# A hybrid layer's first 512 tokens: half of the weight's columns first, squares on ACT, sums later, the norm one group later

## The chip, the cores and the metric

One core of a Trainium2 chip runs the whole layer in one launch. Its engines are named as in the profile: PE (TensorE, matrix products; PEld is its weight load), DVE (VectorE), ACT (ScalarE), POOL (GpSimd) and SP (SyncE, which here only issues transfers). The metric is the device time of one execution in microseconds (us), the median of several runs.

## The reference

The layer normalises its input, multiplies it by one combined weight, sends parts of the result through two token mixers (a gated DeltaNet and a dilated window attention), and adds the projected result to the input. Only the first lines bear on the change:

```python
def rms_norm(x, w):
    xf = x.astype(jnp.float32)
    return xf * lax.rsqrt(jnp.mean(xf * xf, axis=-1, keepdims=True) + EPS) * w.astype(jnp.float32)
...
    h = rms_norm(x, norm_w).astype(x.dtype)
    proj = h @ w_in
```

x is 2048 tokens by 1024 channels, the weight 1024 by 4104, all in float32. The stage that changes computes columns 1536 to 2055 of the projection: the 512 columns of z, the gate of the DeltaNet branch, and eight columns for its decay and beta.

## The kernel before

Every product is made of three: an operand is split into a high part in a shorter float format (fp32r) and a low part, the rest; high by high, high by low and low by high are summed in PSUM. The norm's factor per token (rstd) is applied behind the products, when a PSUM bank is read, so the products need not wait for it.

The first stage runs over four blocks of 512 tokens (tb 0 to 3); x comes in transposed, in pieces of 128 channels by 512 tokens. Piece n is block n // 8, channels of step kt = n % 8. The 520 columns of the weight are taken in two halves of 260 (b 0 and 1), each in eight row blocks of 128 channels.

The helpers of the stage, lines 243 to 320:

- `z_load(kt)` loads a row block of the weight, all 520 columns, into one of four raw buffers (lines 239 and 240: row block kt + 4 comes into the buffer of row block kt). `z_high(kt, b)` casts a half of it to its high part on ACT (`wh`), `z_low(kt, b)` makes the low part on DVE (`wl`).
- `x_in(n)` loads a piece of x into one of six buffers (`xr`), so it waits until piece n - 6 has been read by all. `x_high(n)` on ACT and `x_low(n)` on DVE make its parts (`xh`, `xl`). `x_square(n)` squares it, on POOL for block 0 and on ACT for the others, into `acc` (step 0 of a block) or into one of two buffers `sq`; `x_add(n)` adds that to `acc` on DVE.
- `parts(n)` is square, high part, sum, low part of piece n, and the load of piece n + 6.
- `x_norm(tb)` sums `acc` over the channels with eight small products on PE (`pm`), then DVE (`ssq`) and POOL (`rstd`, a power) make the factor. `x_row` transposes it on PE and copies it (`rr`), `x_row_out` writes it out and reads it back for later stages. All of these use the one PSUM bank `pm`.
- `z_out` reads a finished bank through Silu on ACT with the factor as its scale into one of five buffers (`zt`), copies the eight extra columns on DVE for b = 1 (`ba`), and stores `zt` by a transfer that SP issues (`zs_d`).

The opening, lines 326 to 349, makes the products of tokens 0 to 511 with the half b = 0: eight steps of twelve products (four token tiles, three products each) in four banks, kept open over all steps. Within a step the second half's parts are made too, for row blocks 0 to 3, since their buffers are wanted for row blocks 4 to 7:

```python
    for kt in range(KT):
        x_high(kt)
        z_low(kt, 0)
        x_low(kt)
        if kt + 1 < KT:
            z_high(kt + 1, 0)
        x_square(kt)
        x_add(kt)
        if kt < 4:
            z_high(kt, 1)
            z_low(kt, 1)
            z_load(kt + 4)
```

Then come 28 groups of 24 products (lines 354 to 384), each one bank: groups 0 to 3 are tokens 0 to 511 with b = 1, groups 4 to 11 are block 1 with b = 0 and 1, and so on. With the groups 0 to 3 go two pieces of x each (pieces 8 to 15), with the others one. Groups 1 and 2 use two banks of another pool (`pj`), all others five banks in turn (`pz`), so group 3 needs the bank that token tile 0 had in the opening. In block 0 the norm stands behind the products of group 0 and the first `z_out` behind those of group 1; the banks wait in a list until then.

From line 222 to line 388 every engine's queue, SP's among them, keeps the order in which the lines are written (`pin`); behind line 388 a scheduler sets the order. All transfers spoken of here but one are issued by SP, in order, and an issue that waits for its buffer holds those behind it. Fourteen warm-up products (line 230) run ahead of the first ones.

Of the kernel before, what the change touches and what calls it, by code (L numbers as in the profile page):

```python
# [8 lines left out]
F32 = mybir.dt.float32  # L9
F32R = mybir.dt.float32r  # L10
AF = mybir.ActivationFunctionType
ALU = mybir.AluOpType
# [4 lines left out]
P = 128  # L17
S = 2048
D = 1024
KT = 8  # L20
# [61 lines left out]
def dap(t, off, dims):  # L82
    return bass.AP(tensor=t.tensor, offset=t.offset + off, ap=[list(d) for d in dims])


def hybrid(tc, xT, x, norm_w, w_in, conv_w, a_log, dt_bias, dn_norm_w, q_norm_w, k_norm_w,
# [37 lines left out]
    dma = nc.sync.dma_start  # L124
    adma = nc.scalar.dma_start

    dr, _ = pool("dr", space=DRAM)
# [18 lines left out]
    cst, _ = pool("cst")  # L146
# [34 lines left out]
    wp, wp_g = pool("wp", side="right")  # L181
# [15 lines left out]
    def proj_tok(ps, ws, tt, n, c0=0):  # L197
        tb, o = divmod(tt, 4)
        jobs = [(kt, x_, w_) for kt in range(KT) for x_, w_ in ((xh, 0), (xh, 1), (xl, 0))]
        for j, (kt, x_, w_) in enumerate(jobs):  # L200
            w = ws[kt][w_][:, ws[kt][2], :n]
            nc.tensor.matmul(ps[:, c0:c0 + n], x_[tb][:, kt, o * P:(o + 1) * P], w, start=j == 0, stop=j == len(jobs) - 1)
# [14 lines left out]
    sp0, sp0_g = pool("sp0")  # L217
# [5 lines left out]
    nc = engines  # L223
    dma = nc.sync.dma_start
# [5 lines left out]
    for _ in range(14):  # L230
# [4 lines left out]
    zw = {(b, g): tuple((wp if b + g < 2 else sp0).tile([P, 4, 260], F32R, name=n if b + g < 2 else n + "z",  # L235
                                                        bufs=3 if b + g < 2 else 1) for n in ("wh", "wl"))
          for b, g in ((0, 0), (0, 1), (1, 0), (1, 1))}
    wz = [[(*zw[b, kt // 4], kt % 4) for kt in range(KT)] for b in range(2)]
    raws = [wp.tile([P, 4, 260], F32, name="wraw", bufs=2).rearrange("p (k b) n -> p k (b n)", k=2) for _ in range(2)]
    raws = [raws[k // 2 % 2][:, k % 2] for k in range(KT)]  # L240
    xraw, acc = {}, {}

    def z_load(kt):
        dma(raws[kt], w_in[kt * P:(kt + 1) * P, 1536:2056])

    def z_high(kt, b):
        nc.scalar.activation(zw[b, kt // 4][0][:, kt % 4], raws[kt][:, b * 260:(b + 1) * 260], AF.Copy)

    def z_low(kt, b):
        wh, wl = zw[b, kt // 4]  # L250
        nc.vector.tensor_tensor(wl[:, kt % 4], raws[kt][:, b * 260:(b + 1) * 260],
                                wh[:, kt % 4].bitcast(F32), op=ALU.subtract)

    def x_in(n):
        tb, kt = divmod(n, KT)
        if n < 4 * KT:
            xraw[n] = xr = sp0.tile([P, 512], F32, name="xr", bufs=XRB)
            last_x[0] = dma(xr, xT[kt * P:(kt + 1) * P, tb * 512:(tb + 1) * 512])

    def x_high(n):  # L260
        tb, kt = divmod(n, KT)
        nc.scalar.mul(xh[tb][:, kt], xraw[n], nw[:, kt:kt + 1])

    def x_square(n):
        tb, kt = divmod(n, KT)
        if kt == 0:
            acc[tb] = sq = sp0.tile([P, 512], F32, name="acc", bufs=2)
        else:
            acc[tb, kt] = sq = sp0.tile([P, 512], F32, name="sq", bufs=2)
        if tb == 0:  # L270
            nc.gpsimd.tensor_tensor(sq, xraw[n], xraw[n], op=ALU.mult)
        else:
            nc.scalar.activation(sq, xraw[n], AF.Square)

    def x_low(n):
        tb, kt = divmod(n, KT)
        nc.vector.scalar_tensor_tensor(xl[tb][:, kt], xraw[n], nw[:, kt:kt + 1], xh[tb][:, kt].bitcast(F32),
                                       op0=ALU.mult, op1=ALU.subtract)

    def x_add(n):  # L280
        tb, kt = divmod(n, KT)
        if kt:
            nc.vector.tensor_tensor(acc[tb], acc[tb], acc.pop((tb, kt)), op=ALU.add)

    def parts(n):
        if n < 4 * KT:
            x_square(n)
            x_high(n)
# [12 lines left out]

    def x_row(tb):

        pr = psA.tile([P, 512], F32, name="pm", bufs=1)
        nc.tensor.transpose(pr[:4, :P], rstd[:, 4 * tb:4 * tb + 4], ident)
        rr = sp0.tile([4, P], F32, name="rr")
        nc.vector.tensor_copy(rr, pr[:4, :P])
        return rr

    def x_row_out(tb, rr):  # L310
        dma(dap(rstd_d, tb * 512, [[P, 4], [1, P]]), rr)
        dma(rstd_b[:, tb * 512:(tb + 1) * 512], dap(rstd_d, tb * 512, [[0, P], [1, 512]]))

    def z_out(tt, b, ps):
        zt = sp0.tile([P, 260], F32, name="zt", bufs=5)
        n = 260 if b == 0 else 252
        nc.scalar.activation(zt[:, :n], ps[:, :n], AF.Silu, scale=rstd[:, tt:tt + 1])
        if b:
            nc.vector.tensor_scalar(ba[:, :, tt], ps[:, 252:260], rstd[:, tt:tt + 1], None, op0=ALU.mult)
        dma(zs_d[tt * P:(tt + 1) * P, b * 260:b * 260 + n], zt[:, :n])  # L320

    XRB = 6
    last_x = [None]

    pz = [psZ.tile([P, 512], F32, name="pz", bufs=5) for _ in range(4)]
    for kt in range(4):
        z_load(kt)
        x_in(kt)
    x_in(4)
    z_high(0, 0)  # L330
    for kt in range(KT):
        x_high(kt)
        z_low(kt, 0)
        x_low(kt)
        if kt + 1 < KT:
            z_high(kt + 1, 0)
        x_square(kt)
        x_add(kt)
        if kt < 4:
            z_high(kt, 1)  # L340
            z_low(kt, 1)
            z_load(kt + 4)
        if kt == 0:
            x_in(5)
        x_in(kt + XRB)
        for i in range(4):
            for j, (x_, w_) in enumerate(((xh, 0), (xh, 1), (xl, 0))):
                nc.tensor.matmul(pz[i][:, :260], x_[0][:, kt, i * P:(i + 1) * P], wz[0][kt][w_][:, kt % 4, :260],
                                 start=kt == 0 and j == 0, stop=kt == KT - 1 and j == 2)
# [2 lines left out]
    waiting = [(i, 0, pz[i]) for i in range(4)]  # L352
    n = KT
    for g, (tb, b, i) in enumerate(groups):
        if g == 0:
            for kt in range(4, KT):
                z_high(kt, 1)
                z_low(kt, 1)
        if g in (1, 2):
            ps = psA.tile([P, 512], F32, name="pj", bufs=PJB)  # L360
        else:
            ps = psZ.tile([P, 512], F32, name="pz", bufs=5)
        proj_tok(ps, wz[b], 4 * tb + i, 260)
        for _ in range(2 if tb == 0 else 1):
            parts(n)
            n += 1
        k = g if tb == 0 else (g - 4) % 8
        if k == 0:
            x_norm(tb)
        if k >= 1:  # L370
            for w in waiting:
                z_out(*w)
            waiting = []
        waiting.append((4 * tb + i, b, ps))
        if k == 2:
            rr = x_row(tb)
        if k == 3:
            x_row_out(tb, rr)
        if g == 6:
            dma(cw, conv_w)  # L380
            for w, src in enumerate((q_norm_w, k_norm_w)):
                for s_ in range(2):
                    dma(qw[s_ * CH:(s_ + 1) * CH, w:w + 1], dap(src, 0, [[1, CH], [1, 1]]))
            dma(dnw, dap(dn_norm_w, 0, [[1, P], [1, 1]]))
    for w in waiting:
        z_out(*w)
    nc.vector.tensor_scalar(qw[:, 1:2], qw[:, 1:2], 8.0, None, op0=ALU.mult)
    pin[0] = False
    nc = tc.nc
    dma = nc.sync.dma_start  # L390
# [9 lines left out]
    def small(name):  # L400
# [15 lines left out]
                            op=ALU.add)  # L416
# [455 lines left out]
    nc = engines  # L872
    dma = nc.sync.dma_start
# [455 lines left out]
    for i, g in enumerate(G):  # L1329
        b = 12 * i  # L1330
# [14 lines left out]
        if i < 7:  # L1345
# [215 lines left out]
    g = G[7]  # L1561
# [68 lines left out]
```

## Time and profile before

| | |
|---|---|
| median of 3 runs | 1378.18 us (1377.33 to 1379.85) |
| the profiled execution | 1378.29 us, its span 1376.5 us |
| mean granted PE clock | 0.998 |
| moved by DMA | 205.00 MB, 149 GB/s over the span |
| 50 to 112 us (the groups of products): PE, DVE, ACT busy | 62.00, 22.91, 26.14 of 62.00 us |
| 112 to 212 us (conv projections): PE, DVE, ACT busy | 100.00, 64.02, 42.40 of 100.00 us |

The page gives each engine's busy time and its share of the span. A view by stretches gives, for every stretch of the span: its bounds, its length, then the busy time and the number of instructions (x) of PE, PEld, DVE, ACT and POOL, the granted PE clock, the busy share of the 16 DMA engines, and GB/s; a view of one engine shows that engine alone. In the timelines a line is start, duration, engine, line of the program, operation, what it writes <- what it reads, shapes, count; a bracket says how long the engine had stood idle and what released it. Line 100 is the helper through which all pinned instructions are issued. Durations include an instruction's latency: back to back, the next one starts before the last has ended, and from start to start is what it costs its engine. The chain follows back, from the last instruction, what released each.

### The profile page before, as it was taken

How to read it: one execution, taken by the hardware profiler on the slowest of the kernel's cores; microseconds unless marked ns; L12 is line 12 of the kernel's file. 1: busy time of each engine (PE TensorE's matmuls, PEld its weight loads, DVE VectorE, ACT ScalarE, POOL GpSimd, SP SyncE). 2: the span in 40 equal slices, each digit the busy share in tenths (PEclk: the TensorE clock that was granted, in tenths of full speed). 3: DMA queues.
4: the chain of work that ended last, by engine and by line, in shares of the span. 5: the costliest groups of instructions: out<-in, count | busy, mean ns of one | idle time of the engine just before them, and what ended most of it. 6: DMA issues, size and time to landing. Idle time of an engine off the chain costs nothing.

```text
span 1376.5 us, 28779 instructions
## 1 busy us (share of the span) xinstructions
PE 1361.3 (99%) x10262; PEld 1218.0 (88%) x10262; DVE 835.6 (61%) x2660; ACT 695.0 (50%) x1994; POOL 486.7 (35%) x572
## 2 busy tenths in 40 slices
PE   8999999999999999999999999999999999999998
PEld 7998787778888889999999999999998888888877
DVE  7534668789752356677676575535455746455565
ACT  5644525563322244555555476666666655555520
POOL 3000000000670303443342433583858384655600
PEclk9999999999999999999999999999999999999999
DMA  6654526756637855645744555264648785655773
GB/s 191 187 105 91 111 54 146 156 132 115 116 70 157 176 150 141 157 124 153 197 116 117 108 140 143 77 187 97 178 122 242 198 261 153 200 164 176 201 207 141
DMA packets 301322, 205.00 MB, mean 149 GB/s; under 512 B 149323, under 2 KB 271067, under 8 KB 300668
## 3 DMA queue, kind: packets, MB, share of 16 engines
q1 hardware_dynamic: 230652, 171.09, 49.6%
q10 hardware_dynamic: 70528, 32.09, 8.5%
q8 instruction: 81, 1.33, 0.4%
q14 instruction: 61, 0.50, 0.1%
HBM read 142.61 MB, written 60.50 MB: 148 GB/s over the span
## 4 chain that ended last, share of the span: by engine, by line
PE 86%; DVE 6%; DMA 4%; ACT 2%; issue 1%; POOL 0%; SPq 0%; ACTq 0%; DVEq 0%
PE pj L100 17%; PE po L100 11%; PE sc L100 8%; PE pj L209 7%; PE pj L212 7%; PE pj L211 7%; PE pz L100 6%; PE pv L100 5%; PE pt L100 5%; PE C L736 2%; PE SU L752 2%; PE pm L100 1%; PE C L759 1%; PE A L673 1%; PE A L715 1%
## 5 line engine op out<-in xcount | busy, mean ns | idle before, releaser
L100 PE MATMUL pj<-wh,xh 128*128 128x256 f32 (+1 forms) x776 | 226.6, 292 | 1.4 <-ACT wh L100 1.1
L100 PE MATMUL pj<-wl,xh 128*128 128x256 f32 (+1 forms) x776 | 226.6, 292 | 0.9 <-DVE wl L100 0.9
L100 ACT ACTIVATE pr<-pr,ml 128x192 f32<-128x192 f32 (+2 forms) x384 | 156.9, 410 | 139.6 <-DVE ml L100 134.1
L100 PE MATMUL pj<-wh,xl 128*128 128x256 f32 (+1 forms) x776 | 224.8, 290 | 0.0
L212 PE MATMUL pj<-xh,wl 128*128 128x512 f32 x512 | 203.5, 397 | 0.8 <-DVE wl L193 0.8
L209 PE MATMUL pj<-xh,wh 128*128 128x512 f32 x512 | 202.8, 396 | 0.1
L211 PE MATMUL pj<-xl,wh 128*128 128x512 f32 x512 | 202.4, 395 | 0.0
L100 PE MATMUL po<-xh,mh 128*128 128x512 f32 x424 | 147.9, 412 | 1.0 <-ACT mh L100 0.6
L100 PEld LDWEIGHTS pj<-wh,xh 128*128 128x128 f32 x776 | 146.5, 189 | 1.9 <-ACT wh L100 1.3
L100 PEld LDWEIGHTS pj<-wl,xh 128*128 128x128 f32 x776 | 146.7, 189 | 1.4 <-DVE wl L100 1.3
L100 DVE CUSTOM_DVE_ANT_0 pr<-sc,bias 128x192 f32<-128x192 f32 (+2 forms) x384 | 100.7, 308 | 76.1 <-PE sc L100 72.4
L100 PEld LDWEIGHTS pj<-wh,xl 128*128 128x128 f32 x776 | 146.6, 189 | 0.1
L482 DVE SCALAR_TENSOR_TENSOR cy<-cu,cw,cy 128x512 f32<-128x512 f32 x144 | 111.4, 774 | 19.3 <-ACT cy L480 17.3
L212 PEld LDWEIGHTS pj<-xh,wl 128*128 128x128 f32 x512 | 96.2, 188 | 23.5 <-DVE wl L193 1.2
L100 DVE COPY pT<-pt 64x128 f32<-64x128 f32 (+2 forms) x220 | 69.4, 323 | 76.9 <-PE pt L100 73.4
L209 PEld LDWEIGHTS pj<-xh,wh 128*128 128x128 f32 x512 | 96.4, 188 | 22.1 <-DVE cu L478 0.5
L211 PEld LDWEIGHTS pj<-xl,wh 128*128 128x128 f32 x512 | 96.2, 188 | 22.1
L100 POOL COPY qz<-q 64x512 f32<-64x512 f32 x96 | 94.7, 986 | 47.0 <-PE sc L100 33.8
L547 POOL MEMSET inv<- 128x1024 f32 x1 | 1.0, 956 | 260.1 <-ACT wh L192 260.1
L100 POOL TENSOR_TENSOR Fb<-Fb,op 128x256 f32<-128x256 f32 x84 | 71.9, 869 | 56.9 <-DMA Fb<-F 28.8
L100 PEld LDWEIGHTS po<-xh,mh 128*128 128x128 f32 x424 | 78.0, 189 | 14.1 <-DVE mh L100 1.2
L100 PE MATMUL po<-xl,mh 128*128 128x512 f32 x212 | 86.4, 408 | 0.0
(371 smaller groups left out, 3062.4 us busy)
## 6 DMA issues: line engine op xcount, KB each, us to landing
wraw<-in_w_in SPq DMA_DIRECT2D x44, 512.0 KB, 7.2
cv<-cy ACTq DMA_DIRECT2D x48, 256.0 KB, 2.6
Fb<-F SPq DMA_DIRECT2D x64, 192.0 KB, 5.3
xr<-in_xT SPq DMA_DIRECT2D x32, 256.0 KB, 4.2
kT<-cv SPq DMA_DIRECT2D x32, 256.0 KB, 3.7
qk<-qs ACTq DMA_DIRECT2D x64, 128.0 KB, 3.3
res<-in_x SPq DMA_DIRECT2D x13, 512.0 KB, 4.9
V<-v_d SPq DMA_DIRECT2D x20, 256.0 KB, 4.1
```

Source lines behind the costliest of these rows:

```text
L100: i = f(*args, **kw)
L209: gate_m.append(nc.tensor.matmul(ps, wh[:, k, c * P:(c + 1) * P], xh[tb][:, kt, :], start=kt == 0, stop=False))
L211: nc.tensor.matmul(ps, wh[:, k, c * P:(c + 1) * P], xl[tb][:, kt, :], start=False, stop=False)
L212: nc.tensor.matmul(ps, wl[:, k, c * P:(c + 1) * P], xh[tb][:, kt, :], start=False, stop=kt == KT - 1)
L482: nc.vector.scalar_tensor_tensor(y, u[:, i:i + 512], cw[:, ct, i:i + 1], y, op0=ALU.mult, op1=ALU.add)
L547: eng.memset(Tt, 0.0)
L673: nc.tensor.matmul(pq[:, u], kT[:, u].rearrange("p s i -> p (s i)"), qT[:, u].rearrange("p s i -> p (s i)"), start=True, stop=True)
L715: nc.tensor.matmul(pu[:, u], TT[:, u], kV[:, u], start=True, stop=True)
L736: mark[pair, c, 0] = nc.tensor.matmul(pc[:, s_], g["WQ"][:, u, s_], S0[:, s_], start=True, stop=True)
L752: mark[pair, c, 1] = nc.tensor.matmul(su[:, s_], g["Ks"][:, u, s_], VN, start=True, stop=True)
L759: mark["pe"] = nc.tensor.matmul(po, g["at"][:, u], VN, start=True, stop=True)
```

## The change

The weight's buffers now hold halves of 260 columns: eight half blocks at once, all of b = 0, and each half of b = 1 comes into the buffer that the half of b = 0 had. So there are sixteen loads of half the width instead of eight. The eight first halves and six pieces of x are issued ahead of the steps. In step kt stand the high and low part of x and the weight's half b = 0, the square of the piece before on ACT (block 0's squares leave POOL) and the sum of the piece two before; SP issues the loads of b = 1 (two in step 1, then one a step) ahead of the next piece of x. The last step holds the eighth load, the parts of all eight halves of b = 1, and the squares and sums that are left. There are three `sq` buffers instead of two, and four `zt` buffers instead of five. The norm of block 0 stands behind group 1 instead of group 0, its first `z_out` behind group 2, its row behind group 3, written out in group 4. Blocks 1 to 3 keep their places.

```diff
-    raws = [wp.tile([P, 4, 260], F32, name="wraw", bufs=2).rearrange("p (k b) n -> p k (b n)", k=2) for _ in range(2)]
-    raws = [raws[k // 2 % 2][:, k % 2] for k in range(KT)]
+    raws = [wp.tile([P, 4, 260], F32, name="wraw", bufs=2) for _ in range(2)]
+    raws = {(k, b): raws[k // 4][:, k % 4] for b in range(2) for k in range(KT)}
...
-    def z_load(kt):
-        dma(raws[kt], w_in[kt * P:(kt + 1) * P, 1536:2056])
+    def z_load(kt, b):
+        dma(raws[kt, b], w_in[kt * P:(kt + 1) * P, 1536 + b * 260:1796 + b * 260])
...
-            acc[tb, kt] = sq = sp0.tile([P, 512], F32, name="sq", bufs=2)
-        if tb == 0:
-            nc.gpsimd.tensor_tensor(sq, xraw[n], xraw[n], op=ALU.mult)
-        else:
-            nc.scalar.activation(sq, xraw[n], AF.Square)
+            acc[tb, kt] = sq = sp0.tile([P, 512], F32, name="sq", bufs=3)
+        nc.scalar.activation(sq, xraw[n], AF.Square)
...
-        zt = sp0.tile([P, 260], F32, name="zt", bufs=5)
+        zt = sp0.tile([P, 260], F32, name="zt", bufs=4)
...
-    for kt in range(4):
-        z_load(kt)
-        x_in(kt)
-    x_in(4)
+    for kt in range(KT):
+        z_load(kt, 0)
+        if kt < XRB:
+            x_in(kt)
     z_high(0, 0)
     for kt in range(KT):
         x_high(kt)
...
         x_low(kt)
         if kt + 1 < KT:
             z_high(kt + 1, 0)
-        x_square(kt)
-        x_add(kt)
-        if kt < 4:
-            z_high(kt, 1)
-            z_low(kt, 1)
-            z_load(kt + 4)
-        if kt == 0:
-            x_in(5)
-        x_in(kt + XRB)
+            if kt:
+                x_square(kt - 1)
+            if kt > 1:
+                x_add(kt - 2)
+        else:
+            z_load(kt, 1)
+            for k in range(KT):
+                z_high(k, 1)
+                z_low(k, 1)
+            for k in (KT - 2, KT - 1):
+                x_square(k)
+                x_add(k - 1)
+            x_add(KT - 1)
+        if kt >= 1:
+            for k in ((0, 1) if kt == 1 else (kt,))[:KT - 1 - kt and 2]:
+                z_load(k, 1)
+            x_in(kt + XRB - 1)
+        if kt == KT - 1:
+            x_in(kt + XRB)
...
-        if g == 0:
-            for kt in range(4, KT):
-                z_high(kt, 1)
-                z_low(kt, 1)
...
-        if k == 0:
+        if k == (1 if tb == 0 else 0):
             x_norm(tb)
-        if k >= 1:
+        if k >= (2 if tb == 0 else 1):
             for w in waiting:
                 z_out(*w)
             waiting = []
         waiting.append((4 * tb + i, b, ps))
-        if k == 2:
+        if k == (3 if tb == 0 else 2):
             rr = x_row(tb)
-        if k == 3:
-            x_row_out(tb, rr)
+        if g == 4 or tb and k == 3:
+            x_row_out(g > 4 and tb, rr)
```

More of the change, by code (lines that the diff above doesn't have):

```diff
@@ L238, in hybrid @@
     wz = [[(*zw[b, kt // 4], kt % 4) for kt in range(KT)] for b in range(2)]
-    raws = [wp.tile([P, 4, 260], F32, name="wraw", bufs=2).rearrange("p (k b) n -> p k (b n)", k=2) for _ in range(2)]
-    raws = [raws[k // 2 % 2][:, k % 2] for k in range(KT)]
+    raws = [wp.tile([P, 4, 260], F32, name="wraw", bufs=2) for _ in range(2)]
+    raws = {(k, b): raws[k // 4][:, k % 4] for b in range(2) for k in range(KT)}
     xraw, acc = {}, {}
-    def z_load(kt):
-        dma(raws[kt], w_in[kt * P:(kt + 1) * P, 1536:2056])
+    def z_load(kt, b):
+        dma(raws[kt, b], w_in[kt * P:(kt + 1) * P, 1536 + b * 260:1796 + b * 260])
     def z_high(kt, b):
-        nc.scalar.activation(zw[b, kt // 4][0][:, kt % 4], raws[kt][:, b * 260:(b + 1) * 260], AF.Copy)
+        nc.scalar.activation(zw[b, kt // 4][0][:, kt % 4], raws[kt, b], AF.Copy)
     def z_low(kt, b):
         wh, wl = zw[b, kt // 4]
-        nc.vector.tensor_tensor(wl[:, kt % 4], raws[kt][:, b * 260:(b + 1) * 260],
+        nc.vector.tensor_tensor(wl[:, kt % 4], raws[kt, b],
                                 wh[:, kt % 4].bitcast(F32), op=ALU.subtract)
```

## The prediction

> **What bounds the kernel now.** I read the page first, then the busy time by stretch, the chain of waits in the opening, and each engine's order in time.
>
> ```profile
> span 1376.5 us, 28779 instructions
> PE 1361.3 (99%) x10262; PEld 1218.0 (88%) x10262; DVE 835.6 (61%) x2660; ACT 695.0 (50%) x1994; POOL 486.7 (35%) x572
> ```
> ```profile
> 0.00:50.00 50.00, 45.04 (x314) 42.67 (x315) 35.87 (x64) 30.56 (x61) 13.10 (x15) 0.93 0.68 196
> 50.00:100.00 50.00, 50.00 (x421) 49.95 (x420) 19.62 (x40) 21.95 (x42) 2.39 (x2) 1.00 0.58 128
> ```
> PE (the first busy time behind the length) idles 15.2 us of the span, 5.0 of them in the first 50. Right behind there is no pause, and 10.2 us are spread over the other 1326: what the opening saves on PE's way should come off the end, one for one.
>
> ```profile
> 22.98 1.53 DVE xl L100
> 24.55 5.94 PE pz L100 x46
> 30.49 0.79 PE pm L100 x8
> 43.73 5.87 PE pz L100 x48
> ```
> Up to 24.55 DVE leads the chain, behind it PE. A product takes 5.87/48 = 0.122 us, a group of 24 takes 2.93, a step of 12 takes 1.47. Group 0 ends at 30.49, where the sums of the norm begin (0.79); group 5 has issued its last product at 43.73 + 2.93 = 46.66.
>
> ```profile
> 17.45 1.60 DVE L100 TENSOR_TENSOR wl<-wraw,wh 128x260 fp32r<-128x260 f32 x2
> ...
> 20.24 0.42 DVE L100 TENSOR_TENSOR wl<-wraw,wh 128x260 fp32r<-128x260 f32 x1
> 20.58 1.52 DVE L100 SCALAR_TENSOR_TENSOR xl<-xr,nw,xh 128x512 fp32r<-128x512 f32 x1
> ...
> 22.63 0.42 DVE L100 TENSOR_TENSOR wl<-wraw,wh 128x260 fp32r<-128x260 f32 x1
> ...
> 25.02 0.41 DVE L100 TENSOR_TENSOR wl<-wraw,wh 128x260 fp32r<-128x260 f32 x1
> 25.36 0.74 DVE L100 SCALAR_TENSOR_TENSOR xl<-xr,nw,xh 128x512 fp32r<-128x512 f32 x1
> 26.02 0.68 DVE L100 TENSOR_TENSOR acc<-acc,sq 128x512 f32<-128x512 f32 x1
> 26.62 1.43 DVE L100 TENSOR_TENSOR wlz<-wraw,whz 128x260 fp32r<-128x260 f32 x4
> ```
> ```profile
> 20.39 1.16 POOL L100 TENSOR_TENSOR sq<-xr 128x512 f32<-128x512 f32 x1 [1.63 <-DVE acc L100]
> 31.55 1.40 POOL L100 TENSOR_TENSOR rstd<-ssq,mhalf 128x4 f32<-128x4 f32 x1 [7.61 <-DVE ssq L100]
> ```
> A DVE step of before runs from start to start: 20.24 - 17.45 = 2.79 us with two low halves, 22.63 - 20.24 = 2.39 with one. With no square on POOL the same work is 0.34 (25.02 to 25.36) + 0.66 + 0.60 (to 26.62) = 1.60: each POOL square that runs beside DVE stretches a DVE instruction by 0.78 (0.74 to 1.52).
>
> **The change, opening.** The squares go to ACT, the second halves of the weight out of the steps. DVE per step: 1.60. ACT's prices:
>
> ```profile
> 16.48 0.42 ACT L100 ACTIVATE wh<-wraw 128x260 fp32r<-128x260 f32 x1 [0.61 <-DMA wraw<-in_w_in]
> ...
> 32.98 1.94 ACT L100 ACTIVATE zt<-pz,rstd 128x260 f32<-128x260 f32 x5 [2.38 <-POOL rstd L100]
> ...
> 38.09 0.47 ACT L100 ACTIVATE zt<-pj,rstd 128x252 f32<-128x252 f32 x1 [0.91 <-DMA zs_d<-zt]
> 38.46 0.62 ACT L100 ACTIVATE sq<-xr 128x512 f32<-128x512 f32 x1
> 38.98 0.71 ACT L100 ACTIVATE xh<-xr,nw 128x512 fp32r<-128x512 f32 x1
> 39.59 0.62 ACT L100 ACTIVATE sq<-xr 128x512 f32<-128x512 f32 x1
> ```
> A square holds ACT 0.52, a high part of x 0.61, a high half of the weight at most 0.42: at most 1.55 a step, hidden under DVE's 1.60, as PE's 1.47 is. With that cover gone ACT would set the pace at the same price. The third square buffer lets the sums run two steps late, off the products' path.
>
> The transfers start the opening and, I think, end it:
>
> ```profile
> 2.00:8.00 6.00, 5.66 (x31) 5.31 (x31) 1.24 (x2) 2.25 (x6) 2.06 (x2) 1.00 0.94 211
> 8.00:11.00 3.00, 1.74 (x11) 1.18 (x9) 2.69 (x3) 2.98 (x8) 2.26 (x2) 1.00 0.98 365
> 11.00:24.50 13.50, 11.31 (x60) 10.00 (x60) 13.50 (x20) 6.66 (x16) 5.80 (x5) 0.75 0.73 215
> 114.00:120.00 6.00, 6.00 (x28) 4.85 (x27) 0.92 (x3) 0.30 (x3) 0.00 (x0) 1.00 0.73 136
> ```
> ```profile
> wraw<-in_w_in SPq DMA_DIRECT2D x1, 260.0 KB, 4.1
> ```
> ```profile
> xr<-in_xT SPq DMA_DIRECT2D x1, 256.0 KB, 2.9
> ```
> ```profile
> zs_d<-zt SPq DMA_DIRECT2D x1, 130.0 KB, 3.6
> ```
> The last two numbers of a stretch are the DMA engines' share and GB/s; the three single transfers stand each for the only issue of its stretch. Of the 2.9 us of a lone x I put 1.3 behind its last byte (an estimate: 0.72 is data at 365 GB/s, the rest stands before and behind). A half of the weight is now 0.133 MB instead of 0.266, so x1 ends at byte 0.79 MB: 2.0 + 0.79/0.211 = 5.7, landed 7.0. High part 0.71, low part 0.74: 8.5. Five more steps put low part 6 at 16.5, and low half 7 at 17.5. Only then can SP issue the second half of row block 7: it goes into the buffer that low half 7 has read. Before, a weight load waited in the same way for the low half four steps earlier, and the x behind it on SP with it; that stays, and costs nothing while 14 transfers are queued ahead.
>
> When does that last half land? By its issue: 17.5 + 3.6 to 4.1 (the two 130 to 260 KB rows) = 21.1 to 21.6. By bytes: 16 halves and 12 x ahead are 5.28 MB; 1.27 are through at 8.0 (6 x 0.211), the other 4.01 take 13.6 at 215/0.73 = 294 GB/s or 10.8 at 372: landed 22.9 or 20.1. I take 22.2, between issue and the 294. The rows of 1,040 bytes are the unknown: the conv weights, 1,024 bytes a row, ran at 136/0.73 = 186 GB/s (114 to 120). With halves at that rate and x at 294: 11.4 + 10.7 + 2.0 + 1.3 = 25.4. Ends kept: 21.1 and 25.4. High and low half 0.42 each behind it: T = 23.1 is where the last low half is ready and group 0 can finish (T + 0.4 = 23.5, against 30.49: 7.0 us ahead).
>
> **The change, behind T.** All that was put off now stands in DVE's and ACT's queues. DVE: three sums (1.8), then for x8 to x11 four low parts and three sums (4.44), then the norm's sum: T + 6.3, rstd 1.40 later, first zt at T + 8.2 = 31.3. PE: group 1 to 26.4, norm 27.2, group 2 to 30.1; group 3 needs the bank that the first zt frees: a wait of 1.2 us, which PE did not have.
>
> The norm's delay also puts six zt into one flush, with four buffers (five before). The 0.91 us above is this wait in the kernel before, at one zt.
>
> ```profile
> 34.03 0.33 SPq L100 DMA_DIRECT2D xr<-in_xT  x1
> 34.41 1.91 SPq L100 DMA_DIRECT2D zs_d<-zt  x4
> ```
> On SP the first store stands behind the load of x19, which waits for low part 13: T + 8.9 (two low parts and two sums more). Plus 0.38 for that issue, store landed 3.6 later: T + 12.9. The fifth zt starts there, the sixth 0.48 later (one issue), and ACT is free at T + 13.8. Behind it in ACT's queue stand square and high part of x14 and x15 (2 x 1.13, the last with its 0.71): T + 16.15; on DVE the last low part, T + 16.9. Group 4, entered at 34.25, has products for six blocks (2.2 us) and then waits from 36.45 to about 40.1, with six products in between: 2.9 us lost. Before leaving,
>
> ```profile
> 38.73 0.27 DVE L100 COPY rr<-pm 4x128 f32<-4x128 f32 x1
> ...
> 41.66 0.23 DVE L100 TENSOR_SCALAR ba<-pj,rstd 128x8 f32<-128x8 f32 x1
> ```
> these two (at most 0.5 together, 0.3 beyond the last products) hold the next norm's bank. Norm 0.79, group 5: T + 21.1 = 44.2 against 46.66.
>
> The sum: 7.0 - 1.2 - 2.9 - 0.4 = 2.5 us gained. The profiled execution took 1378.29 (span 1376.5 and 1.8 around it), 0.1 above the median: 1375.8. The whole hangs on T, one for one: 21.1 gives 1374.7, 25.4 gives 1379.0. From group 5 on the loops are as before. The order behind line 388 is the scheduler's; I know no row for a shift there and give it 1 us either way (an estimate).
>
> **Rivals.** *Full passage*: the store or low part 13 is early enough that group 4 doesn't wait. Then 2.9 more comes through, 1372.9; without the wait at group 3 too, 1371.3. For it: before, ACT waited only 0.91 us. Against: one buffer fewer, and the x loads ahead on SP. I take 1372.
>
> *The clock gate closes in group 4.*
>
> ```profile
> 5.84:12.66 6.82, 4.82 (x32) 1.00 0.94 261
> 12.66:19.49 6.83, 6.36 (x27) 0.50 0.78 237
> 19.49:26.32 6.83, 5.47 (x40) 1.00 0.56 167
> ```
> ```profile
> 11.40 0.39 PE L100 MATMUL pz<-wh,xl 128*128 128x260 f32 x1 [1.06 <-DVE xl L100]
> ```
> After 6.82 us with PE busy for 4.82, no single wait over 1.06, the granted clock was 0.50 for 6.83 us; after 5.47 busy it stayed. Waiting 2.9 in such a stretch leaves about 3.9 busy. The price is half of 6.83, 3.4 us: 1379.2, if the stretch falls so.
> The Trainium skill, "TensorE: Matmul & The Clock Gate", section "Why this matters for your kernels", asks for no idle gaps over about 3 us between bursts; my longest single gap is 1.7, so by it the gate stays open and the time is 1375.8. The 1.06 us row speaks against reading it so.
>
> *The queue is the bound (slower).* Halved rows and 14 waiting transfers keep the rate of 2 to 8 us, 211/0.94 = 224 GB/s: 5.28/0.224 + 3.3 = 26.9, T = 27.8, 1380.5; at 186 GB/s throughout it is 1385.3. I take 1382. It turns slower than before from a landing at 24.7. Against it: 365 GB/s from 8 to 11, with the queue just as full.
> The Trainium skill, "DMA: Bandwidth & Descriptors", section on measured bandwidth, puts a transfer of 64 KB at 32% of its peak and one of 1 MB at 78%. Here eight of 260 KB become sixteen of 130, so by it this rival is nearer than I have it; the trace's 365 GB/s, made of 260 KB transfers in a full queue, disagrees.
>
> *The steps don't get shorter*, since ACT takes POOL's place: no, 1.55 is under 1.60; under 1 in 50.
>
> **How the numbers follow.** Forecast 0.47, full passage 0.17, gate 0.20, queue 0.13, others 0.03. A measurement tells about 0.2% from no change, 2.8 us. The forecast's own range, 1374.0 to 1379.0, lies half beyond that limit (T under 22.8): faster 0.23 + 0.17 = 0.40; within: 0.24 + 0.20 + 0.02 = 0.46; slower: 0.14. The range runs from full passage, 1371.3, to gate and late landing, 1380.0.
>
> **What would show it.** Right: POOL without squares, DVE steps of 1.6, group 0's end near 23.5, PE waits of about 1.2 in group 3 for a zt and about 2.9 in group 4 for xl, ACT's fifth zt waiting some 3 us for a store. Wrong: group 4 without a wait, group 0 past 26, a clock of 0.50 behind 30, or the gain lost behind 50.

## The result, and the profile after

The changed kernel takes 1386.69 us (median of 4 runs, 1385.41 to 1387.55) against 1378.26 us (median of 4, 1377.33 to 1379.85): a ratio of 1.0053 [1.0040, 1.0066]. It is slower by 8.4 us where 2.5 us less had been forecast, and it lies 6.7 us above the upper end of the range. The profiled execution took 1385.41 us.

The page of the changed kernel:

```profile
span 1383.4 us, 28801 instructions
PE 1364.4 (99%) x10262; PEld 1221.5 (88%) x10262; DVE 832.0 (60%) x2660; ACT 699.1 (51%) x2002; POOL 474.7 (34%) x564
```

POOL has eight instructions fewer, ACT eight more. The view by stretches says where the time went; from left to right after the length: PE, PEld, DVE, ACT, POOL, PE's granted clock, the DMA engines' share, GB/s.

```profile
0.00:50.00 50.00, 41.00 (x266) 38.39 (x267) 28.74 (x59) 31.47 (x62) 3.33 (x7) 0.91 0.71 181
50.00:100.00 50.00, 50.00 (x402) 49.96 (x401) 21.02 (x41) 23.32 (x44) 2.05 (x2) 0.95 0.58 132
```

In the first 50 us PE is busy 41.00 instead of 45.04, and in both stretches the clock falls below 1.00. The chain of waits in order of time (start, us, what):

```profile
7.08 7.32 DMA wraw<-in_w_in
...
14.64 7.05 DMA xr<-in_xT
...
22.18 4.24 DMA wraw<-in_w_in
26.44 0.43 ACT whz L100
26.89 0.43 DVE wlz L100
...
38.49 5.27 DMA zs_d<-zt
...
47.40 1.61 PE pm L100 x8
49.00 8.56 PE pz L100 x48
57.67 17.31 PE pz L100 x144
```

The same place in the chain of the kernel before:

```profile
42.95 0.79 PE pm L100 x8
43.73 5.87 PE pz L100 x48
49.71 17.25 PE pz L100 x144
```

Three things stand in the changed kernel's chain that the chain before did not have: loads that take over 7 us (a half block of the weight, then a piece of x), the wait for a store of z (the chain follows a later one of its six stores), and 48 products in 8.56 us instead of 5.87. At the last row of both it is 57.67 - 49.71 = 8.0 us behind, and so it stays: the first product of the convolutions' stage comes at 119.98 instead of 112.00, and from there to the end the two kernels take the same (median less that point: 1266.7 and 1266.3 us). So everything happens in the first 58 us.

**The loads.** The first stretches of the opening:

```profile
2.00:8.00 6.00, 6.00 (x33) 6.00 (x33) 1.61 (x3) 2.50 (x6) 1.02 (x1) 1.00 0.99 165
8.00:11.00 3.00, 2.70 (x20) 2.28 (x19) 1.42 (x3) 2.27 (x6) 0.00 (x0) 1.00 1.04 263
11.00:14.00 3.00, 2.72 (x22) 2.51 (x22) 2.56 (x6) 2.73 (x6) 0.00 (x0) 1.00 1.02 187
14.00:17.00 3.00, 2.65 (x20) 2.22 (x19) 2.68 (x5) 2.27 (x5) 0.00 (x0) 1.00 1.02 111
17.00:20.00 3.00, 1.26 (x10) 1.06 (x9) 0.70 (x2) 0.57 (x2) 0.00 (x0) 1.00 1.04 364
```

The DMA engines are busy all the time (0.99 to 1.04) and yet move as little as 111 GB/s, halves of the weight and pieces of x together. By 14.0 that is 2.34 MB (6 x 0.165 + 3 x 0.263 + 3 x 0.187); the forecast had 3.03 there (1.27 + 6 x 0.294). Who waits for it, in the order of ACT and then of DVE (start, duration, engine; in brackets the idle time before and its releaser):

```profile
19.65 0.72 ACT L100 ACTIVATE xh<-xr,nw 128x512 fp32r<-128x512 f32 x1 [2.43 <-DMA xr<-in_xT]
```
```profile
17.27 0.42 DVE L100 TENSOR_TENSOR wl<-wraw,wh 128x260 fp32r<-128x260 f32 x1
20.41 0.75 DVE L100 SCALAR_TENSOR_TENSOR xl<-xr,nw,xh 128x512 fp32r<-128x512 f32 x1 [2.71 <-ACT xh L100]
21.08 0.68 DVE L100 TENSOR_TENSOR acc<-acc,sq 128x512 f32<-128x512 f32 x1
21.68 0.42 DVE L100 TENSOR_TENSOR wl<-wraw,wh 128x260 fp32r<-128x260 f32 x1
```

The piece that ACT waits for until 19.65 is x6: it was issued at 12.30 and took about 7.3 us. Low part 6 of x ends at 21.16 instead of 16.5, low half 7 at 22.10 instead of 17.5. The last half load is issued right behind it, at 22.18, and T is 26.89 + 0.43 = 27.32.

**The store and the clock.** The timelines of ACT, SP and PE, and the store's transfer (last number: us from issue to landing):

```profile
35.54 1.58 ACT L100 ACTIVATE zt<-pz,rstd 128x260 f32<-128x260 f32 x4 [0.83 <-POOL rstd L100]
42.70 0.47 ACT L100 ACTIVATE zt<-pz,rstd 128x252 f32<-128x252 f32 x1 [5.58 <-DMA zs_d<-zt]
```
```profile
30.20 6.71 SPq L100 DMA_DIRECT2D xr<-in_xT  x6
36.97 7.02 SPq L100 DMA_DIRECT2D zs_d<-zt  x6
```
```profile
zs_d<-zt SPq DMA_DIRECT2D x1, 130.0 KB, 5.6
```
```profile
36.07 0.39 PE L100 MATMUL pz<-wh,xh 128*128 128x260 f32 x1 [1.11 <-ACT zt L100]
...
41.20 0.28 PE L100 MATMUL pz<-wh,xl 128*128 128x260 f32 x1
44.76 0.58 PE L100 MATMUL pz<-wh,xh 128*128 128x260 f32 x1 [3.28 <-ACT xh L100]
...
47.20 1.81 PE L100 MATMUL pm<-one,acc 128*128 128x1 f32 x8
```
```profile
44.65:54.90 10.25, 10.02 (x42) 9.34 (x43) 6.11 (x13) 6.23 (x14) 1.38 (x1) 0.50 0.43 131
```

The first zt comes at T + 8.2. The store stands on SP behind six loads of x, as foreseen, but lands 5.6 us after its issue, so the fifth zt starts at 42.70. PE stands still for 3.28 us in group 4, and as it goes on, the granted clock is 0.50 for 10.24 us: what is left of group 4, the norm's sums and group 5 run at half speed (group 6, from 54.9 on, at full speed again).

### The profile page after: what moved, and what is told of

It reads as the page before. It is cut to its first block, busy times and chain, and to the rows that moved or that the text cites. A ratio compares the mean times of both kernels' runs of the same rounds, so it can differ in the third digit from the quotient of the medians.

```text
span 1383.4 us, 28801 instructions
## 1 busy us (share of the span) xinstructions
PE 1364.4 (99%) x10262; PEld 1221.5 (88%) x10262; DVE 832.0 (60%) x2660; ACT 699.1 (51%) x2002; POOL 474.7 (34%) x564
## 4 chain that ended last, share of the span: by engine, by line
PE 83%; DMA 5%; DVE 5%; ACT 4%; issue 2%; POOL 1%; SPq 0%; ACTq 0%; DVEq 0%
PE pj L100 16%; PE po L100 11%; PE sc L100 8%; PE pj L209 7%; PE pj L212 7%; PE pj L211 7%; PE pz L100 5%; PE pv L100 5%; PE pt L100 5%; PE C L739 2%; PE SU L755 2%; DMA wraw<-in_w_in 1%; PE pm L100 1%; PE A L676 1%; PE C L762 1%
```

## The experiments

My theory after these views: three costs in a row, which the prediction had as one term and two rivals. (A) The halved rows of the weight, 1,040 bytes each and 16,416 bytes apart, are read slowly, and T comes 4 us late. (B) Six zt with four buffers make ACT wait for a store, and through ACT's queue PE. (C) That wait shuts the clock gate. The rivals are named in the expectations. A kernel called "from the changed one" or "from the one before" has only the edit that is shown. "Stage end" is the first convolution product in the profiled execution, one for each kernel; "behind" is the median less that; the ratio is to the kernel before in runs on the same chip (its medians there: 1379.24, 1379.75 and 1379.69 us, so its own "behind" lies between 1266.3 and 1267.8).

| run | edit | median us | ratio [95%] | stage end | behind |
|---|---|---|---|---|---|
| before | | 1378.26 | | 112.00 | 1266.3 |
| after | the change | 1386.69 | 1.0053 [1.0040, 1.0066] | 119.98 | 1266.7 |
| e3_packed | after, rows next to each other | 1382.94 | 1.0028 [1.0018, 1.0037] | 114.04 | 1268.9 |
| e10_pitch2080 | after, rows 2,080 bytes apart | 1383.71 | 1.0028 [1.0015, 1.0041] | 113.56 | 1270.2 |
| e11_pitch8224 | after, rows 8,224 bytes apart | 1381.43 | 1.0020 [1.0009, 1.0031] | 113.82 | 1267.6 |
| e2_zt_raw | after, a buffer for each store | 1378.47 | 0.9994 [0.9985, 1.0003] | 110.72 | 1267.8 |
| e5_fill | after, 14 products in the wait | 1387.18 | 1.0059 [1.0040, 1.0079] | 115.86 | 1271.3 |
| e9_fill10 | after, 10 products in the wait | 1386.45 | 1.0054 [1.0039, 1.0069] | 117.05 | 1269.4 |
| e6_packed_zt_raw | after, e3 and e2 together | 1374.50 | 0.9954 [0.9939, 0.9969] | 106.25 | 1268.3 |
| e1_norm_back | after, norm at its old place | 1382.91 | 1.0024 [1.0015, 1.0033] | 114.37 | 1268.5 |
| e12_norm_back_zt_raw | after, e1 and e2 together | 1381.66 | 1.0012 [1.0002, 1.0022] | 114.00 | 1267.7 |
| e4_sq_act | before, squares on ACT | 1376.04 | 0.9978 [0.9968, 0.9987] | 109.54 | 1266.5 |
| e8_sq_act_packed | before, squares on ACT, rows packed | 1374.83 | 0.9951 [0.9934, 0.9967] | 106.74 | 1268.1 |
| e7_one_more | before, one product more | 1379.67 | 0.9997 [0.9987, 1.0006] | 112.20 | 1267.5 |

**The rows (A).** e3_packed reads the halves from a copy of these columns, in which the 1,040-byte rows of a half lie next to each other; the copy is laid out ahead of the launch and its making is not in the time. e10 and e11 do the same from copies with other distances; among the three copies only the distance of the rows differs.

```diff
# e3_packed, from the changed kernel
-        dma(raws[kt, b], w_in[kt * P:(kt + 1) * P, 1536 + b * 260:1796 + b * 260])
+        dma(raws[kt, b], w_z[(b * KT + kt) * P:(b * KT + kt + 1) * P, :])
# e10_pitch2080: w_z is 1024 x 520
+        dma(raws[kt, b], w_z[kt * P:(kt + 1) * P, 0 + b * 260:0 + 260 + b * 260])
# e11_pitch8224: w_z is 1024 x 2056
+        dma(raws[kt, b], w_z[kt * P:(kt + 1) * P, 1536 + b * 260:1536 + 260 + b * 260])
```

> The changed kernel, but the sixteen half loads read from a packed copy of the 520 columns, laid out ahead of the launch: rows of 1,040 bytes one behind the other instead of 16,416 bytes apart. Theory 1 (scattered rows of the weight are what keeps the DMA engines busy at 111 to 220 GB/s): the stretch 2 to 17 us moves at 300 GB/s or more, the last weight load lands near 21.5 instead of 26.4, and 4 to 5 us come off, more if the gate then stays open: 1378 to 1382.5. Theory 2 (the first 17 us are slow whatever is loaded, or it is the number of transfers): loads as before, 1385.5 to 1387.5.

> The changed kernel with its half loads read from a copy of the 520 columns alone: rows of 1,040 bytes, 2,080 bytes from one to the next instead of 16,416 (and 1,040 in the packed run). Theory (rows near each other are what is fast): packets and stage as in the packed run, norm near 26, stage end 110 to 114.5. Rival (only rows without a gap are fast): as the changed kernel, norm near 31, stage end 119 to 120.

> The same with rows 8,224 bytes apart, about the distance of x's rows (8,192). Theory A (the cost grows with the distance): between the two, norm at 27.5 to 30. Theory B (any distance beyond a few rows costs the same): as the changed kernel, norm near 31. Theory C (8 KB is near enough, as x's rows seem to show): norm near 26.

The opening by stretches, of e3_packed, of e10_pitch2080 and of e11_pitch8224:

```profile
2.00:8.00 6.00, 6.00 (x35) 6.00 (x35) 2.61 (x5) 3.66 (x8) 1.02 (x1) 1.00 0.89 262
...
14.00:17.00 3.00, 3.00 (x25) 2.79 (x24) 3.00 (x7) 3.00 (x7) 0.00 (x0) 1.00 0.94 303
```
```profile
2.00:8.00 6.00, 6.00 (x36) 6.00 (x36) 2.52 (x5) 3.65 (x8) 1.02 (x1) 1.00 0.88 263
...
14.00:17.00 3.00, 3.00 (x24) 2.77 (x23) 3.00 (x7) 3.00 (x9) 0.00 (x0) 1.00 1.00 318
```
```profile
2.00:8.00 6.00, 6.00 (x33) 6.00 (x33) 2.63 (x5) 3.65 (x8) 1.02 (x1) 1.00 0.92 236
...
14.00:17.00 3.00, 3.00 (x25) 2.76 (x24) 3.00 (x7) 2.62 (x6) 0.00 (x0) 1.00 1.03 342
```

With the same loads in the same order, 236 to 263 GB/s stand where 165 stood, and 303 to 342 where 111 stood. So it is neither the halved size of a transfer nor gaps between rows as such: of the four distances only that of the weight itself, 16,416 bytes, is slow, and 8,224 is already fast. (A copy with the old distance was not run, so the weight's place in memory is not ruled out as a part of it.) DVE in e3_packed, low part 6 and low half 7:

```profile
15.55 0.74 DVE L100 SCALAR_TENSOR_TENSOR xl<-xr,nw,xh 128x512 fp32r<-128x512 f32 x1
16.81 0.42 DVE L100 TENSOR_TENSOR wl<-wraw,wh 128x260 fp32r<-128x260 f32 x1
```

They end at 16.29 and 17.23, where the prediction had 16.5 and 17.5: with these rows its opening comes true. The norm begins at 24.99 to 26.11 instead of 31.02, and the stage ends 5.9 to 6.4 us sooner; by the ratios the whole gains less, 3.4 to 4.6 us, and e3_packed's median lies just above what its theory expected. The wait for the store stays: in all three the clock is halved for 6.8 us from 40.5 to 41.3 on.

**The stores (B) and the clock (C).** e2_zt_raw gives the eight stores of the first four token tiles buffers of their own, out of two that the weight has left by then; e5_fill and e9_fill10 keep the wait and put products of a zero tile with itself into group 4's bank while PE waits (they add zero).

```diff
# e2_zt_raw, from the changed kernel
-        zt = sp0.tile([P, 260], F32, name="zt", bufs=4)
+        if tt < 4:
+            if not spare:
+                two = [wp.tile([P, 4, 260], F32, name="wraw", bufs=2) for _ in range(2)]
+                spare.extend(t[:, i] for t in two for i in range(4))
+            zt = spare.pop(0)
+        else:
+            zt = sp0.tile([P, 260], F32, name="zt", bufs=4)
# e5_fill, from the changed kernel (e9_fill10: 10 instead of 14)
+            if j == 18:
+                for _ in range(fill):
+                    nc.tensor.matmul(ps[:, :P], rstd_b[:, :P], rstd_b[:, :P], start=False, stop=False)
...
-        proj_tok(ps, wz[b], 4 * tb + i, 260)
+        proj_tok(ps, wz[b], 4 * tb + i, 260, fill=14 if g == 4 else 0)
```

> The changed kernel with one thing taken away: the eight z stores of the first 512 tokens come out of the eight raw weight buffers, which are free by then, so no zt waits for a store. Theory (a late last weight load, then the wait of ACT for a store with four buffers, then the clock gate that closes in the wait of group 4): ACT's 5.6 us wait goes, low part 15 is ready near 40.5, group 4 runs through, the granted clock stays 1.00 behind 30, and group 6 ends near 49 instead of 57.6: about 9 us less, 1377 to 1379. Rival (the late loads alone set the time, the store wait is hidden behind them or taken over by the next wait): 1384 to 1387.

> The changed kernel with 14 products of zeros (0.2 us each at full clock) added into group 4's bank between its sixth and seventh row block, where PE waits 3.3 us; the result is unchanged. Theory (the gate closes because of that wait): the clock stays 1.00 behind 30; the 10.2 us at half clock go, of which about 4 are lost work: 1382 to 1383.5. Rival (the gate closed for what lay before, or the half clock is hidden): 0.50 still shows behind 44 and the time is 1386 to 1387, or longer by what the filling adds.

> The changed kernel with ten products of zeros in group 4 instead of the fourteen of the earlier run, so that the gate stays open and the scheduler sees yet another time. At the end of the stage, as before: 115.9, about 4.1 ahead of the changed kernel. Theory (the earlier run lost its 4 us behind the stage to waits and a half clock of that program or those executions, not to anything that filling does): the time keeps most of the 4 us, 1382 to 1384. Rival (keeping the gate open in group 4 is paid back later in any case): 1386 to 1388 again.

Of e2_zt_raw, ACT's second part of the flush, the only wait of PE between 34 and 43 us, and the stretch in which the changed kernel had half the clock:

```profile
36.78 0.50 ACT L100 ACTIVATE wraw<-pj,rstd 128x252 f32<-128x252 f32 x1
```
```profile
35.50 0.39 PE L100 MATMUL pz<-wh,xh 128*128 128x260 f32 x1 [0.74 <-ACT wraw L100]
```
```profile
44.65:54.90 10.25, 10.25 (x88) 10.23 (x87) 5.67 (x10) 6.50 (x13) 0.00 (x0) 1.00 0.47 146
```

ACT goes through its six reads without a pause, group 4 waits for nothing, the clock stays full there: the stage ends 9.3 us sooner, the total falls by 0.59% of the time before (1.0053 to 0.9994), 8.1 us, and is no longer to be told from before. Of e5_fill and of e9_fill10, what is left of PE's wait, and the same stretch:

```profile
44.15 0.39 PE L100 MATMUL pz<-wh,xh 128*128 128x260 f32 x1 [0.16 <-ACT xh L100]
```
```profile
44.65:54.90 10.25, 9.55 (x75) 9.03 (x75) 6.82 (x15) 8.04 (x16) 1.39 (x1) 1.00 0.54 146
```
```profile
43.82 0.39 PE L100 MATMUL pz<-wh,xh 128*128 128x260 f32 x1 [1.03 <-ACT xh L100]
```
```profile
44.65:54.90 10.25, 9.84 (x64) 9.31 (x65) 5.30 (x12) 6.64 (x14) 1.39 (x1) 0.83 0.53 156
```

With the wait filled the clock is full there, though the fifth zt still waits 5.62 us for the store; the stage ends 4.1 us sooner than in the changed kernel. With four products fewer 1.03 us are left open, the clock is halved for 3.4 us from 47.98 on, and the stage ends 2.9 us sooner instead of 4.1.

How the 9.3 us of e2_zt_raw divide is read at the norm's sums of block 1. They begin at 41.48 instead of 47.20, so 5.7 us lie ahead of them (0.6 of these already ahead of the wait: group 3 goes on at 35.50 instead of 36.07), and 3.5 us behind them, where the clock is now full. In e5_fill it is 0.7 ahead (46.52) and 3.4 behind. So the half clock is worth about 3.5 us, and the wait about 5.

That the total would fall by as much did not come true in either: the medians of e5_fill and of e9_fill10 are even with the changed kernel's, where their rivals had them, though the half clock that e5_fill's rival had behind 44 us did not come. Where e5_fill loses its 4 us again, the profiled executions show in part: behind the stage it takes 4.4 us more than the changed kernel (1267.8 and 1263.4 us of the spans). A half clock of 3.4 us at 462 is 1.7 of them. And PE stands still there for 12.2 us instead of 10.0, 1.8 of them in one wait for a load (`yt`) that the changed kernel does not have. What brings these is open. The half clock of e9_fill10 at 819 says nothing of the filling: PE has the same two waits there in all fourteen profiled executions (1.07 to 1.14 and 0.87 to 0.88 us, one product between them), and in seven of them, e3, e4, e8, e9, e10, e11 and e12, the clock is halved for 3.4 us behind these waits, in the other seven not.

**Both together.** e6_packed_zt_raw joins the two edits.

> The changed kernel with both causes taken away: the half loads from a packed copy of the columns, and the first eight z stores out of the raw weight buffers. Theory (the two are all that stands between the change and its gain, and add up): the norm begins near 26 instead of 31, nothing waits behind it for long, the stage ends near 105.5 (before 112.0, changed 119.98): 1371.5 to 1374.5. Rival (with them gone, DVE's backlog of sums or ACT takes their place): stage end 108 or later, 1375 or more.

The stage ends at 106.25, 13.7 us sooner than in the changed kernel, and no stretch of the execution has a halved clock but its last 1.3 us. The total is 1374.50. So the two causes carry all that the change lost, and nearly add up (5.9 and 9.3 apart, 13.7 together). What is left is a gain of 5.8 us at the stage end and 0.46% of the total.

**The norm's place.** e1_norm_back sets norm, flush and row of block 0 back to where they stood; e12_norm_back_zt_raw does that to e2_zt_raw.

```diff
-        if k == (1 if tb == 0 else 0):
+        if k == 0:
             x_norm(tb)
-        if k >= (2 if tb == 0 else 1):
+        if k >= 1:
...
-        if k == (3 if tb == 0 else 2):
+        if k == 2:
...
-        if g == 4 or tb and k == 3:
-            x_row_out(g > 4 and tb, rr)
+        if k == 3:
+            x_row_out(tb, rr)
```

> The changed kernel with one part undone: the norm of the first 512 tokens, its first flush and its row stand one group earlier again, as in the kernel before; loads, squares, sums and the four zt buffers as changed. Theory (the late norm is not what costs: the last weight load at 26.4 puts DVE's sums late, and the fifth zt waits for a store in either place): PE now waits for the sums ahead of the norm, the fifth zt stands in the flush behind group 1 and still waits some 5 us for a store: the stage ends within 1.5 us of the changed kernel's 119.98, the time is 1385 to 1388. Rival (the six zt in one flush are what makes the store wait matter): 1378 to 1381.

> The changed kernel without the store wait (the z stores of the first 512 tokens out of the raw buffers) and with the norm back at its old place. It tells what the norm's delay costs or brings when no store waits. Theory (the norm's delay mattered only through the sixth zt and the store it waits for): stage end within 1.5 us of the 110.72 of the run without the store wait, 1377 to 1379.5. Rival (the late norm costs by itself): stage end 108.5 or earlier, 1375 to 1377.

The first time lies between what the two sides expected, and the second went against my theory. With four buffers the late norm costs 5.6 us at the stage end (119.98 against 114.37), 4.0 by the ratios: put back, the first store is issued at 34.74 and lands 3.5 us later, PE waits only 0.63 us in group 4, and the clock is full there (it is halved for 3.4 us from 31.96 on, behind a wait of 1.25 us for the sums). With buffers enough the late norm saves 3.3 us (110.72 against 114.00), 2.5 by the ratios. PE's timeline of e12_norm_back_zt_raw, and its stretch from 29.3 on, show what it saves:

```profile
29.05 1.64 PE L100 MATMUL pm<-one,acc 128*128 128x1 f32 x8 [1.78 <-DVE acc L100]
```
```profile
29.30:36.10 6.80, 6.80 (x32) 6.80 (x33) 5.56 (x11) 6.22 (x14) 1.39 (x1) 0.50 0.62 205
```

The sums, now two steps late, are not ready when group 0 ends; PE waits 1.78 us for them, and the clock is halved for 6.8. Moving the norm is right, then, but it must come with the buffers that its larger flush needs. How many would do was not run: the change also took the fifth zt buffer away, and no run has the late norm with five or six.

**The squares alone.** e4_sq_act moves only the squares of block 0 to ACT; e8_sq_act_packed also reads the weight's 520 columns from a copy with rows next to each other (2,080 bytes a row).

```diff
# e4_sq_act, from the kernel before
-        if tb == 0:
-            nc.gpsimd.tensor_tensor(sq, xraw[n], xraw[n], op=ALU.mult)
-        else:
-            nc.scalar.activation(sq, xraw[n], AF.Square)
+        nc.scalar.activation(sq, xraw[n], AF.Square)
```

> The kernel before with one part of the change alone: the squares of the first 512 tokens on ACT instead of POOL; loads, sums, norm and buffers as before. Theory: without POOL's squares a DVE step takes 1.94 (two low halves) or 1.60 instead of 2.79 and 2.39, and the wide loads keep up for most of it: group 0 ends 4 to 6 us earlier and nothing behind it waits anew: 1372.5 to 1374.5. Rival 1 (loads bind as soon as DVE is faster): 1375 to 1377. Rival 2 (the same later waits as in the changed kernel): 1378 or more.

> The kernel before with the squares of the first 512 tokens on ACT (as in the run that gave 1376.0), and its eight full-width loads read from a packed copy of the 520 columns, rows of 2,080 bytes one behind the other. Theory (scattered rows bind there too: ACT waited twice for 4.7 us on a weight load): group 0 ends near 25.5 instead of 27.9, the stage at 107 to 107.5 instead of 109.5: 1373 to 1375. Rival (DVE's two low halves a step bind, the loads were hidden): 1375.5 to 1377.

DVE and ACT in e4_sq_act:

```profile
17.80 0.42 DVE L100 TENSOR_TENSOR wl<-wraw,wh 128x260 fp32r<-128x260 f32 x1
18.14 0.74 DVE L100 SCALAR_TENSOR_TENSOR xl<-xr,nw,xh 128x512 fp32r<-128x512 f32 x1
18.80 0.68 DVE L100 TENSOR_TENSOR acc<-acc,sq 128x512 f32<-128x512 f32 x1
19.40 0.42 DVE L100 TENSOR_TENSOR wl<-wraw,wh 128x260 fp32r<-128x260 f32 x1
```
```profile
20.94 0.42 ACT L100 ACTIVATE wh<-wraw 128x260 fp32r<-128x260 f32 x1 [1.72 <-DMA wraw<-in_w_in]
```

Here is the step of 1.60 (17.80 to 19.40), where no load is late. But loads are late again and again; the expectation's rival, that they bind, was right. Still, of all versions that read the weight where it lies this is the fastest: 1376.04 us, 0.9978 [0.9968, 0.9987] of the kernel before, so it beats both kernels. With packed rows the stage ends another 2.8 us sooner, as expected: with the squares on ACT the distance of 16,416 bytes costs the old order something, too. (The 4.7 us in that expectation are two loads from issue to landing; ACT itself stood 1.13 and 1.72 us for them.) And with packed rows this version (0.9951) and the mended change (e6_packed_zt_raw, 0.9954) are even: beside the squares, the new order of the opening brings nothing that these runs can tell.

**The order behind line 388.** e7_one_more adds one zero product to group 2 of the kernel before, to see whether any small edit shifts what the scheduler does later.

> The kernel before with one product of zeros more (about 0.2 us) in group 2, which changes nothing in the opening but gives the scheduler other times to order what lies behind line 388. Theory (that order moves the time by itself, as the filled kernel showed: 4.1 us ahead of the changed one at the end of the stage, level with it at the end): the stage ends at 112.2 and the time still differs from before by 1 us or more, to either side. Rival (the order is without weight, the filled kernel lost its gain elsewhere): 1378 to 1380, as before within the measurement.

The ratio is 0.9997 [0.9987, 1.0006], so this one shows no shift, against the theory: -0.4 us, with an interval from -1.8 to +0.8.

## Why the prediction was wrong, step by step

- **What the opening saves or loses comes off the end, one for one.** Right for the change itself: 8.0 us at 57.67, 8.0 at the stage end, 8.4 in the medians. It held less well in the experiments: behind the stage the medians lie between 1266.5 and 1271.3, where the kernel before has 1266.3 to 1267.8. The half clock near 815 us, there in half of the profiled executions, is 1.7 us of that scatter; for the rest I found no rule.
- **DVE's step of 1.60, ACT hidden at 1.55.** The prices were right (0.75 for a low part, and 1.60 measured in e4_sq_act). That DVE sets the pace was not: its steps run 1.79 and 2.00 us (13.48, 15.27, 17.27 are the starts of the low halves), and then it stands for 2.71. In e3_packed it does set it, at 1.60.
- **The step that failed: "Five more steps put low part 6 at 16.5, and low half 7 at 17.5."** It took the queue of 14 transfers to be ahead of the engines. The queue was behind them: low half 7 ended at 22.10. From there the forecast held in the main: the last half landed 4.2 us after its issue (26.4; "landed 22.2" had 4.7), and group 0 ended at T + 0.8, at 28.15, instead of T + 0.4. T is 4.2 late, and e3, e10 and e11 show that it is the rows: with other distances the same step comes out as forecast (17.23 in e3_packed). I had named these rows as the unknown, with 186 GB/s as the lower end, and then taken 294 over the mix; 178 was measured from 2 to 17 us (2.67 MB), 111 in the worst three. Against the rival I held the 365 GB/s of 8 to 11 us. The changed kernel has such a stretch as well (364, from 17 to 20), right behind its slowest one: a peak over 3 us said nothing about the bytes of the whole queue. And the 186 GB/s were no lower end: the stretch of 114 to 120 us also holds the load of a 256 KB constant (`msk`). The same trace of the kernel before has a purer row, two loads of conv weights (rows of 1,024 bytes, 16,416 bytes apart) with a few stores of z:

```profile
73.00:80.00 7.00, 7.00 (x61) 6.97 (x60) 4.17 (x7) 3.72 (x8) 0.00 (x0) 1.00 1.00 96
```

At 96 GB/s the sixteen halves (2.13 MB) alone would take 22 us, by estimate. That is worse than what came, but it puts the late end far behind 25.4.

- **The wait in group 3: 1.2.** Measured 1.11, and the first zt at T + 8.2 as forecast, though the terms that the forecast lists, 6.3 and 1.40, reach only T + 7.7; measured, the norm's sum on DVE stands at T + 6.6 and rstd at T + 6.8.
- **The fifth zt at T + 12.9.** It came at T + 15.4. The mechanism was right (store behind x19 on SP, ACT behind the store, PE behind ACT), and so was the place, low part 13 at T + 9.2 for T + 8.9. Mis-sized was the landing: 5.6 us for 3.6, the only such row that I had. Group 4 ended at T + 19.9 instead of T + 17.0, 2.9 more.
- **The gate.** Priced at 3.4, a chance of 0.20, as a case beside the forecast. But it hung on the same wait, which had grown from 1.7 to 3.28 us in one piece. From the norm's sums to the 144 products the chain takes 57.67 - 47.40 = 10.27 us, before 49.71 - 42.95 = 6.76: 3.5 lost. The Trainium skill, "TensorE: Matmul & The Clock Gate", section "Why this matters for your kernels", asks for no idle gaps over about 3 us: the changed kernel's 3.28 us agrees, e12_norm_back_zt_raw's 1.78 and e9_fill10's 1.03 (with 0.28 and 0.41 behind it) do not fit. Nor does PE's busy time alone: the forecast had the clock stay behind 5.47 busy of 6.83 us, and in e1_norm_back it was halved behind 5.58.
- **The sum.** 4.2 + 2.9 + 3.5 = 10.6 us, and 1375.8 + 10.6 = 1386.4 for 1386.69 measured. The rival of the queue had T at 27.8 (27.3 measured) and yet only 1382, since it kept the store and the open gate of the forecast. But the late loads and the store are two causes that add up (e3_packed, with early loads, still has a store that lands after 5.5 us and a half clock of 6.8), and the gate follows from the store. Treated as alternatives they never came together, and so the range ended at 1380.0.
- **The rule on the size of transfers.** The size rule that the prediction took from the Trainium skill, "DMA: Bandwidth & Descriptors", section "Bandwidth", measured there with transfers issued by GpSimd, pointed to the right rival. But size is not what decided here: e3_packed moves the same 130 KB transfers, with x between them, at 303 GB/s from 14 to 17 us.
- **1 us for the scheduler.** e7_one_more shows no shift beyond -1.8 to +0.8 us, for one edit.
- **What would show it wrong.** Two of the signs named came: group 0 past 26 (28.15), and a clock of 0.50 behind 30.

## What to carry to other kernels

Before a load is split along its rows, work out the bytes of the whole queue at the rate of rows with the same length and the same distance, search the whole trace for such rows in a stretch where little else moves, and if there are none, take the slow end as seriously as the fast one. When a step is put off, count what its flush then does at once: buffers against stores, and what stands ahead of the first store on the issuing queue. And ask of every two rivals whether both can happen: costs that stand one behind the other on the path, or of which one brings the other, are added into one case, and the range reaches to their sum.

## What the runs showed of the hardware

- A queue of halves with rows of 1,040 bytes 16,416 bytes apart, and x between them, moved 111 GB/s (14 to 17 us, the engines' share 1.02), with distances of 1,040, 2,080 and 8,224 bytes 303, 318 and 342. Conv weights with rows of 1,024 bytes at the same distance came at 96 GB/s, stores of z included, at a share of 1.00 (before, 73 to 80 us). The cause in the memory is open; distances between 8,224 and 16,416 were not tried, nor a copy with the old one. The page "DMA: Bandwidth & Descriptors" of the Trainium skill, section "Latency and other measured facts", has row distances that slow a copy, from 2 MiB on; no run here shows those, and 16,416 bytes is not among them.
- In the first 60 us the half clock came for 3.4, 6.8 and 10.24 us, and the longest wait of PE in the 6.8 us ahead of it lay between 1.03 us (e9_fill10) and 3.42 us (e10_pitch2080). Near 815 us the same two waits, about 1.1 and 0.9 us, were followed by a half clock of 3.4 us in seven of fourteen profiled executions: how long PE waits does not settle it alone.
- The first stores of block 0, 130 KB each, land between 3.4 us (e1_norm_back) and 5.8 us (e10_pitch2080) after their issue. In the kernel before, beside the conv weights' loads from 70 to 80 us, the median of three was 10.0. What sets it is not settled.
